# A hybrid encoder layer in split fp32 on one core: weight casts of the first pass placed behind the u of the block ahead, and three late row tiles normalised on GpSimd

## The chip, the core and the metric

The kernel runs on one core of a Trainium2 chip. The metric is the device time of one execution in microseconds (us). Three runs of the kernel before took 689.14, 689.45 and 689.67 us; their median is 689.45 us. A profile of one more execution was taken, and all rows below are from it.

## The reference

One layer with 1024 tokens of width 1024. `c` is a conditioning vector that gives a scale, a shift and a gate.

```python
mod = silu(c) @ w_ada + b_ada                       # shift, scale, gate: 1024 each
u = layer_norm(x) * (1 + scale) + shift             # [1024, 1024]
h = u @ w_in                                        # q, k, v, gate columns of two head groups
...
y = concat(fox(fq, fk, fv, ff) * silu(fg), stick_breaking(sq, sk, sv) * silu(sg)) @ w_out
out = layer_norm(2 ** 0.25 * x + gate * y) * ln_g + ln_b
```

## The kernel before, in words

All matrix products are done on TensorE (PE) with every fp32 operand split into two fp32r parts, a rounded one ("hi", names `uh`, `whi`, the first half of `hw`) and a remainder ("lo", names `ul`, `wlo`, the second half of `hw`); a product is hi·hi + hi·lo + lo·hi, so three matmuls. The order of PE and of the DMA queue on SP is the order of the code. ScalarE (ACT), VectorE (DVE) and GpSimd (POOL) get their order from a scheduler, which `with after(...)` (L83) can hold: an instruction in it is placed behind the ones named.

The width of 1024 is cut into 8 column blocks `kb`, the tokens into 8 row tiles `t` of 128. The rows of `x` are normalised per row tile; after that PE transposes 128x128 pieces so that a block of u lies with its width on the partitions.

**First pass** (L672 to L734, about 12 to 46 us of the span). It works on row tiles 0 to 3 (512 tokens) and goes through the blocks 0 to 7. Five sums grow side by side in PSUM, `st_q0`, `st_k0`, `st_g0`, `st_q1`, `st_k1` (`acc0`). For each block:

- `mod_terms(kb)` (L230): two DVE instructions per block, each the sum over one 128x1024 tile of `w_ada` columns times silu(c). They give `modc`, the scale and the shift of that block. The tiles `wss` are loaded by SP into three buffers.
- `u_turn` (L242): four transposes on PE into the PSUM tile `xT_early`.
- `u_round` (L248, L249): two ACT instructions. The first writes `uh` (rounded), the second puts the full u back into the PSUM tile.
- `u_rest` (L261): DVE writes `ul`, the full u less `uh`. After that `xT_early` is free for the next block's transposes. `in_turn` (L223) keeps the terms and the remainders on DVE in the order of the calls.
- `start_split` (L598, L599): the weights of the block, four pieces of 128 columns: ACT casts `raws` into the hi half of `hw`, POOL subtracts and writes the lo half.
- `start_steps` (L612, L615): PE. For blocks 2 to 6 the order is: eight matmuls that read `uh` (four with weight hi, four with weight lo), the four transposes of the next block, two more with `uh` for the fifth sum, and five with `ul`.

In the loop of block kb, the u of block kb+1 is held behind the ACT cast of the weights of block kb+1 (L685). The weights of block kb+2 are split in the loop of block kb (L706).

**Row tiles 4 to 7** are normalised near the end of the first pass: `norm_stats` (L193 to L211) has two BN_STATS and a BN_AGGR on DVE and two or three 128x1 instructions on POOL, `norm_x` (L214) is one 128x1024 instruction. By `NORM_ON` (L76) tiles 4 and 5 are normalised on ACT (L218), 6 and 7 on DVE (L217).

**Behind the first pass** PE makes the values of head pair 0 for row tiles 0, 1 and 2 (`v_first`, 24 matmuls of 128x256 each, L352 to L354), then the transposes of row tiles 4 to 7 for blocks 0 and 1 (`late_round`, L773), the values of row tile 3, and the **second pass**: the first three sums for tokens 512 to 1023, with u of block kb+2 made two blocks ahead. The values of row tile t are evicted in two halves (L360 on ACT, then L361 on DVE, then the same for the second half). Row tiles 0 and 2 share the PSUM tile `st_late`, so the matmuls of row tile 2 wait for the DVE eviction of row tile 0. The second pass's third sum `st_g0b` takes the PSUM buffer of `st_g0` and waits for its eviction (`evac_g`, L289 on ACT, L290 on DVE).

Then the attention runs with the remaining projections between its steps, and at the end the output projection with the last layer norm.

Of the kernel before, what the change touches and what calls it, by code (L numbers as in the profile page):

```python
# [16 lines left out]
NB = 8  # L17
# [10 lines left out]
def tile_hybrid_layer(  # L28
# [17 lines left out]
    nc = tc.nc  # L46
# [6 lines left out]
    def big(tag, bufs, name, dt=F32, shape=None):  # L53
        return sb.tile(shape or [P, 1024], dt, tag=tag, bufs=bufs, name=name)
# [4 lines left out]
    def pt_tile(name, dt=F32R, shape=None):  # L59
        return big("pt", 3, name, dt, shape or [P, 2, 1024])  # L60
# [12 lines left out]

    RING = 5
    WARM = (4, 1, 1, 0, 0)
    NORM_ON = {6: nc.vector, 7: nc.vector}  # L76
    FLOG = 4
    FROW = 8
    GATE = 10
# [3 lines left out]
    def after(*instructions):  # L83
        stack = ExitStack()
        for i in instructions:
            stack.enter_context(tc.issue_after(i.ins))
        return stack
# [29 lines left out]
    def ring_w(key):  # L117
        return [sb.tile([P, 528], F32R, tag=tag, bufs=RING, name=f"{tag}_{key}") for tag in ("whi", "wlo")]
# [33 lines left out]
    def load_ss(kb):  # L152
        t = sb.tile([P, 2, D], F32, tag="v", bufs=3, name=f"wss_{kb}")
        for a in ((0, 1), (1, 2)) if kb < 6 else ((0, 2),):
            nc.sync.dma_start(t[:, a[0]:a[1], :], w_ss[kb, :, a[0]:a[1], :])
        wss_sb.append(t)
# [38 lines left out]
    def ln_stats(src, name):  # L195
        st = sb.tile([P, 3, 6], F32, tag="st", bufs=3, name=f"st_{name}")[:, :2, :]
        nc.vector.bn_stats(st[:, 0, :], src[:, 0:512])
        nc.vector.bn_stats(st[:, 1, :], src[:, 512:1024])
        return ln_finish(st, name)
# [8 lines left out]
    def norm_stats(t):  # L208
        mv, rs = norm[t] = ln_stats(xt[t], f"a{t}")
        if t not in NORM_ON:  # L210
            nc.gpsimd.tensor_scalar(rs[:, 1:2], mv[:, 0:1], rs[:, 0:1], -1.0, op0=ALU.mult, op1=ALU.mult)  # L211

    def norm_x(t, a=0, b=D):
        mv, rs = norm[t]  # L214
        xs = xt[t][:, a:b]
        if t in NORM_ON:
            return NORM_ON[t].tensor_scalar(xs, xs, mv[:, 0:1], rs[:, 0:1], op0=ALU.subtract, op1=ALU.mult)  # L217
        return nc.scalar.activation(xs, xs, AF.Identity, scale=rs[:, 0:1], bias=rs[:, 1:2])  # L218
# [4 lines left out]
    def in_turn(make, *args):  # L223
        with after(*turn_of):
            turn_of[:] = [make(*args)]
        return turn_of[0]
# [6 lines left out]
    def mod_terms(kb, parts=(0, 1)):  # L233
        for i in parts:
            in_turn(mod_part, kb, i)
# [3 lines left out]
    def u_turn(kb, a=0, b=512, tp=None, tiles=None):  # L239
        tp = xT[kb, a] = tp or t_tile(f"xT_{kb}_{a}")  # L240
        for t in tiles or range(a // P, b // P):
            nc.tensor.transpose(tp[:, t * P - a:t * P - a + P], xt[t][:, kb * P:(kb + 1) * P], ident)  # L242
# [3 lines left out]
    def u_round(kb, a=0, b=512):  # L246
        full = xT[kb, a][:, :b - a]
        nc.scalar.activation(u_hi[kb][:, a:b], full, AF.Identity, scale=modc[:, kb, 0:1], bias=modc[:, kb, 1:2])  # L248
        return nc.scalar.activation(full, full, AF.Identity, scale=modc[:, kb, 0:1], bias=modc[:, kb, 1:2])  # L249

    def u_split(kb):
        full = raw_tile(f"u_full_{kb}")[:, :512]
        psum = xT.pop((kb, 0))[:, :512]
        s, b = (modc[:, kb, i:i + 1] for i in range(2))
        nc.scalar.activation(u_hi[kb][:, :512], psum, AF.Identity, scale=s, bias=b)
        last = nc.scalar.activation(full, psum, AF.Identity, scale=s, bias=b)
        nc.gpsimd.tensor_tensor(u_lo[kb][:, :512], full, u_hi[kb].bitcast(F32)[:, :512], op=ALU.subtract)
        return last
# [54 lines left out]
    def evac_m(p, m, ch, acc, heads=(0, 1)):  # L313
        if m == 0:
            evac_q(p, ch, acc, qst[p], heads)
        elif m == 1:
            return evac_k(p, ch, acc, kst[p], klo[p], heads)
        else:
            evac_g(p, ch, acc, sgt[p])
# [244 lines left out]
    raw_w, split, split_at, used, early_w = {}, {}, {}, [0], []  # L564
# [21 lines left out]
    def start_split(key):  # L586
        if key[0] == "h" or key[1] < 3:
            hi, lo = ring_w("st" + key[0] + str(key[1]))
        else:
            if key[1] == 3:  # L590
                early_w.append(pt_tile("hw_34"))
            elif key[1] == 5:
                early_w.append(pt_tile("hw_56"))
            home = (early_w[-1][:, (key[1] - 3) % 2, :] if key[1] < 7 else big("sg", 2, "hw_7", F32R))
            hi, lo = home[:, :512], home[:, 512:]
        split[key] = hi, lo
        h3, l3 = (t[:, :512].rearrange("p (m c) -> p m c", m=4) for t in (hi, lo))
        split_at[key] = (nc.scalar.copy(h3, raw_w[key]),  # L598
                         nc.gpsimd.tensor_tensor(l3, raw_w[key], h3.bitcast(F32), op=ALU.subtract))  # L599

    def start_steps(ns, accs, kb, a=0, b=512, parts=(0, 1), ends=None):
        first, last = ends or (kb == 0, kb == NB - 1)
        s = slice(a, b)
        w = {}
        for n in ns:
            hi, lo = split[("k", kb) if n < NW else ("h", kb // 4)]
            at = n if n < NW else kb % 4
            w[n] = hi[:, at * P:at * P + P], lo[:, at * P:at * P + P]
        if 0 in parts:
            for i in range(2):  # L610
                for n in ns:
                    nc.tensor.matmul(accs[n], w[n][i], u_hi[kb][:, s], start=(first and i == 0), stop=False)  # L612
        if 1 in parts:
            for n in ns:
                nc.tensor.matmul(accs[n], w[n][0], u_lo[kb][:, s], start=False, stop=last)  # L615
# [25 lines left out]
    rounded = u_split(0)  # L641
# [18 lines left out]
    def v0_load(n):  # L660
        if n == 0:
            home = sb.tile([P, 4, 512], F32R, tag="v", bufs=3, name="v0_home")
            v0_home.update({m: (home[:, 2 * m], home[:, 2 * m + 1]) for m in range(2)})
        v0_raw[n] = start_raw(1)
        nc.sync.dma_start(v0_raw[n], w_v[0, n])
# [6 lines left out]
    for kb in range(NB):  # L672
        last = kb == NB - 1
        if last:
            start_steps(ALL[:2], acc0, kb)
            for n in range(2):
                evac_m(*START[n], 0, acc0[n])
            start_steps(ALL[2:], acc0, kb)
            break
        start_steps(ALL[:4], acc0, kb, parts=(0,))  # L680
        if kb == 0:
            u_turn(2, tp=xt_early)
        elif kb > 1:
            u_turn(kb + 1, tp=xt_early)
        with after(split_at["k", kb + 1][0]):  # L685
            rounded = u_split(kb + 1) if kb == 0 else u_round(kb + 1)
        if kb == 0:
            with after(rounded):
                start_split(("h", 0))
            mod_terms(2)  # L690
        else:
            parts = range(2 if kb + 2 < NB else 0)
            mod_terms(kb + 2, parts[:1])
            rest = in_turn(u_rest, kb + 1)
            mod_terms(kb + 2, parts[1:])
        if kb == 0:
            start_steps(ALL[:4], acc0, kb, parts=(1,))
        elif kb == 1:
            start_steps(ALL[:4], acc0, kb, parts=(1,))
            for k in range(2):  # L700
                start_steps(ALL[4:], acc0, k)
        else:
            start_steps(ALL[4:], acc0, kb, parts=(0,))
            start_steps(ALL, acc0, kb, parts=(1,))
        if kb + 2 < NB:
            start_split(("k", kb + 2))  # L706
        if kb == 2:
            start_split(("h", 1))
        if kb + 5 < NB:
            load_ss(kb + 5)  # L710
            if kb == 0:
                load_w4(6, 2)
        if kb == 2:
            for n in range(2):
                v0_load(n)
            load_x(4)
            for n in range(2, 4):
                v0_load(n)
            for t in range(5, NB):
                load_x(t)  # L720
        if kb == 5:
            with after(*split_at["k", NB - 1]):
                for n in range(4):
                    v0_split(n)
            norm_stats(4)
            norm_stats(5)
            norm_x(4)
            norm_x(5)
        if kb == 6:
            with after(rest):  # L730
                for t in (6, 7):
                    norm_stats(t)
                    norm_x(t)
            make_v(0)  # L734
# [57 lines left out]
    rounded = late_round(1)  # L792
# [4 lines left out]
    for kb in range(NB):  # L797
        if kb + 2 < NB:
            rounded = late_round(kb + 2)
# [338 lines left out]
```

## Time and profile before

| what | value |
|---|---|
| median of three runs | 689.45 us |
| time of the profiled execution | 689.13 us |
| its span | 687.2 us |
| PE busy | 671.8 us (98%) |
| DVE busy | 488.3 us (71%) |
| ACT busy | 381.3 us (55%) |
| POOL busy | 403.2 us (59%) |
| first matmul of the values of row tile 0 | 46.31 us |
| first matmul of the sum `st_g0b` | 60.80 us |

The profiled execution lies 1.93 us above its span, and 0.32 us below the median. A row of the timeline has the start in us from the start of the span, the duration in us, the engine, the line, the operation, what is written from what is read, a count, and in brackets how long the engine had been idle and what released it. PEld is PE's weight load, SPq the issue of a DMA on SP.

### The profile page before, as it was taken

What the parts mean: (1) busy time and instruction counts of PE and PEld (TensorE: products, weight loads), DVE (VectorE), ACT (ScalarE), POOL (GpSimd) and SP (SyncE); (2) the same over time, 40 slices, a digit from 0 to 9 for tenths busy, and PEclk for the clock granted to TensorE, in tenths of its full rate; (3) what the DMA queues carried; (4) which work ended last, traced back from release to release, by engine and by line L of the source; (5) the groups of instructions that cost most, each with busy time, mean ns of one, the idle gap of its engine ahead of it and who ended that gap; (6) DMA issues with size and microseconds to landing.
All of it is one profiled execution on the core that took longest, in us unless ns stands there. A gap on an engine that the chain in (4) does not pass through costs nothing.

```text
span 687.2 us, 11196 instructions
## 1 busy us (share of the span) xinstructions
PE 671.8 (98%) x3709; PEld 571.2 (83%) x3709; DVE 488.3 (71%) x996; ACT 381.3 (55%) x857; POOL 403.2 (59%) x529
## 2 busy tenths in 40 slices
PE   8999999999999999999999999999999999999995
PEld 5788888788998888889988888889988878888885
DVE  6696769968668677777776675766676778785645
ACT  6566377756667666566665564655565666521000
POOL 5650179746447655556369878668785365655411
PEclk9999999999999999999999999999999999999998
DMA  9954422112102112112134455254352297143301
GB/s 335 409 221 170 152 74 76 40 26 55 40 9 70 40 54 55 40 50 58 36 104 128 161 162 166 80 176 146 116 163 72 60 353 300 59 174 106 118 31 61
DMA packets 45272, 81.54 MB, mean 119 GB/s; under 512 B 5216, under 2 KB 19360, under 8 KB 44960
## 3 DMA queue, kind: packets, MB, share of 16 engines
q1 hardware_dynamic: 43632, 76.54, 33.8%
q10 hardware_dynamic: 1584, 4.31, 1.9%
q8 instruction: 29, 0.48, 0.3%
q14 instruction: 27, 0.22, 0.1%
HBM read 60.34 MB, written 16.29 MB: 112 GB/s over the span
## 4 chain that ended last, share of the span: by engine, by line
PE 83%; DVE 6%; DMA 4%; ACT 3%; POOL 2%; issue 2%; DVEq 0%; POOLq 0%; ACTq 0%
PE m L296 9%; PE pv L526 9%; PE m L298 9%; PE m L297 9%; PE T L509 9%; PE S L458 4%; PE S L457 4%; PE o L901 4%; PE o L900 4%; PE o L899 4%; PE v L354 3%; PE v L352 3%; PE v L353 3%; DMA wss<-in_w_ss_dram 3%; PE st_late L612 1%
## 5 line engine op out<-in xcount | busy, mean ns | idle before, releaser
L296 PE MATMUL m<-uh,whi 128*128 128x512 f32 x304 | 125.0, 411 | 0.7 <-DVE kl L284 0.7
L512 DVE TENSOR_TENSOR pt<-T,pt 128x512 fp32r<-128x512 f32 (+2 forms) x192 | 103.1, 551 | 26.0 <-ACT pt L511 24.2
L298 PE MATMUL m<-uh,wlo 128*128 128x512 f32 x304 | 119.7, 394 | 0.0
L297 PE MATMUL m<-ul,whi 128*128 128x512 f32 x304 | 119.6, 394 | 0.0
L511 ACT CAST pt<-T 128x512 fp32r<-128x512 f32 (+2 forms) x192 | 88.6, 478 | 42.0 <-PE T L509 39.1
L492 POOL TENSOR_TENSOR be<-be,kp 128x127 f32<-128x127 f32 (+3 forms) x64 | 77.1, 1204 | 37.2 <-DVE kp L490 27.6
L486 DVE TENSOR_TENSOR_SCAN kp<-kp,floor 128x512 f32<-128x512 f32 (+2 forms) x64 | 65.1, 1018 | 27.6 <-ACT kp L479 25.4
L526 PE MATMUL pv<-pt,v 128*128 128x512 f32 x320 | 82.8, 388 | 0.3 <-DVE pt L512 0.3
L536 POOL TENSOR_TENSOR ty<-ty,sg 64x256 f32<-64x256 f32 x64 | 47.0, 734 | 42.6 <-DVE ty L535 18.3
L473 POOL TENSOR_SCALAR a<-a,l 128x1024 f32<-128x1024 f32 (+3 forms) x64 | 48.2, 752 | 39.7 <-DVE l L471 29.5
L298 PEld LDWEIGHTS m<-uh,wlo 128*128 128x128 f32 x304 | 57.1, 188 | 13.7
L457 PE MATMUL S<-k,q 128*128 128x512 f32 (+5 forms) x192 | 66.2, 346 | 0.2 <-DVE nm L465 0.2
L296 PEld LDWEIGHTS m<-uh,whi 128*128 128x128 f32 x304 | 57.2, 188 | 10.1 <-DVE kl L284 1.1
L458 PE MATMUL S<-kl,qz 128*128 128x512 f32 (+5 forms) x192 | 65.3, 341 | 0.0
L470 ACT ACTIVATE a<-a,nm 128x1024 f32<-128x1024 f32 (+3 forms) x64 | 49.8, 778 | 26.4 <-DVE nm L465 25.8
L297 PEld LDWEIGHTS m<-ul,whi 128*128 128x128 f32 x304 | 57.3, 189 | 7.9
L526 PEld LDWEIGHTS pv<-pt,v 128*128 128x128 f32 x320 | 55.4, 189 | 9.6 <-DVE pt L512 0.6
L479 ACT ACTIVATE kp<-S 128x128 f32<-128x128 f32 (+3 forms) x64 | 41.8, 652 | 33.7 <-PE S L458 31.3
L465 DVE CUSTOM_DVE_ANT_0 a<-S,fb 128x1024 f32<-128x1024 f32 (+3 forms) x64 | 48.2, 754 | 15.8 <-PE S L458 12.4
L431 ACT CAST qz<-q 64x128 fp32r<-64x128 f32 x128 | 37.3, 295 | 34.5 <-PE S L458 33.3
L352 PE MATMUL v<-whi_v,uh 128*128 128x256 f32 (+1 forms) x192 | 55.5, 289 | 0.0
L354 PE MATMUL v<-wlo_v,uh 128*128 128x256 f32 (+1 forms) x192 | 54.3, 283 | 0.3 <-POOL wlo_v L127 0.3
(290 smaller groups left out, 1625.0 us busy)
## 6 DMA issues: line engine op xcount, KB each, us to landing
raw<-in_w_qkg_dram SPq DMA_DIRECT2D x38, 256.0 KB, 2.6
wss<-in_w_ss_dram SPq DMA_DIRECT2D x12, 512.0 KB, 8.4
x<-in_x_dram SPq DMA_DIRECT2D x8, 512.0 KB, 6.8
k<-k SPq DMA_DIRECT2D x32, 128.0 KB, 2.3
wg<-in_w_gate_dram SPq DMA_DIRECT2D x8, 512.0 KB, 4.2
raw_o<-in_w_out_dram SPq DMA_DIRECT2D x16, 256.0 KB, 3.0
fb<-f_dr ACTq DMA_DIRECT2D x8, 512.0 KB, 4.2
wo_dr<-whi_o SPq DMA_DIRECT2D x16, 256.0 KB, 2.2
```

The source lines that it names most:

```text
L296: nc.tensor.matmul(acc, hi[:, c], u_hi[kt][:, s], start=(kt == 0), stop=False)
L297: nc.tensor.matmul(acc, hi[:, c], u_lo[kt][:, s], start=False, stop=False)
L298: nc.tensor.matmul(acc, lo[:, c], u_hi[kt][:, s], start=False, stop=(kt == NB - 1))
L352: nc.tensor.matmul(acc[:, :n], u_hi[kt][:, ts_], hi[:, s], start=(kt == 0), stop=False)
L354: nc.tensor.matmul(acc[:, :n], u_hi[kt][:, ts_], lo[:, s], start=False, stop=(kt == NB - 1))
L457: nc.tensor.matmul(S[:, s, :w], qst[p][h][:, qs], kst[p][h][:, ks], start=True, stop=False)
L458: nc.tensor.matmul(S[:, s, :w], z, klo[p][:, ks], start=False, stop=True)
L486: last_dve = nc.vector.tensor_tensor_scan(rv, rv, floor[:, :ke - lo], initial=0.0, op0=ALU.mult, op1=ALU.max)
L492: nc.gpsimd.tensor_tensor(be[:, :ke - 1], be[:, :ke - 1], kp[:, 1:ke], op=ALU.mult)
L511: nc.scalar.copy(hi[:, :n, qo:qo + P], t3)
L512: lows[:] = [nc.vector.tensor_tensor(lo[:, :n, qo:qo + P], t3, hi.bitcast(F32)[:, :n, qo:qo + P], op=ALU.subtract)]
L526: nc.tensor.matmul(acc2[:, :, q0:], vt[p][:, kb, h * P:(h + 1) * P], pt[:, :, q0:], start=(kb == 0), stop=(kb == last))
```

## The change

```diff
-    NORM_ON = {6: nc.vector, 7: nc.vector}
+    NORM_ON = {t: nc.gpsimd for t in (5, 6, 7)}
...
-        with after(split_at["k", kb + 1][0]):
+        with after(*split_at["k", kb + 1][:1] if kb < 2 else ()):
             rounded = u_split(kb + 1) if kb == 0 else u_round(kb + 1)
...
             parts = range(2 if kb + 2 < NB else 0)
-            mod_terms(kb + 2, parts[:1])
+            late = kb in (3, 4)
+            mod_terms(kb + 2, () if late else parts[:1])
             rest = in_turn(u_rest, kb + 1)
-            mod_terms(kb + 2, parts[1:])
+            mod_terms(kb + 2, parts if late else parts[1:])
...
-        if kb + 2 < NB:
-            start_split(("k", kb + 2))
         if kb == 2:
             start_split(("h", 1))
+        elif kb < 2:
+            start_split(("k", kb + 2))
+        elif kb + 2 < NB:
+            with after(rounded):
+                for k in ((4, 5) if kb == 3 else (kb + 2,)):
+                    start_split(("k", k))
```

Row tiles 5, 6 and 7 are normalised on POOL. From block 3 on, u no longer stands behind a weight cast; the weights of blocks 4 to 7 are split behind the u of the block ahead (4 and 5 behind the u of block 4, 6 behind that of 5, 7 behind that of 6). In the loops of blocks 3 and 4 the remainder (of blocks 4 and 5) stands ahead of both DVE sums of the next block (5 and 6). PE and SP keep their order; ACT, DVE and POOL have another one only between the u of block 4 and the eviction of `st_g0`, and from there on every engine has the same list as before.

Place 1 is ACT in the first pass, from the u of block 4 to that of block 6. The first number in a name is the block or pair (for `hw` the blocks whose weights it holds), the last only a tile's number; `raws_3` holds the weights of blocks 4 and 5, `raws_4` those of 6 and 7. Before:

```order
L598 CAST hw_34_321<-raws_3_248 128x512
L248 ACTIVATE uh_4_128<-xT_early_147,modc_140 128x512
L249 ACTIVATE xT_early_147<-xT_early_147,modc_140 128x512
L598 CAST hw_56_396<-raws_3_248 128x512
L598 CAST hw_56_396<-raws_4_296 128x512
L598 CAST hw_7_449<-raws_4_296 128x512
L248 ACTIVATE uh_5_129<-xT_early_147,modc_140 128x512
L249 ACTIVATE xT_early_147<-xT_early_147,modc_140 128x512
L248 ACTIVATE uh_6_130<-xT_early_147,modc_140 128x512
```

And now:

```order
L248 ACTIVATE uh_4_128<-xT_early_147,modc_140 128x512
L249 ACTIVATE xT_early_147<-xT_early_147,modc_140 128x512
L598 CAST hw_34_321<-raws_3_248 128x512
L598 CAST hw_56_396<-raws_3_248 128x512
L248 ACTIVATE uh_5_129<-xT_early_147,modc_140 128x512
L249 ACTIVATE xT_early_147<-xT_early_147,modc_140 128x512
L598 CAST hw_56_396<-raws_4_296 128x512
L248 ACTIVATE uh_6_130<-xT_early_147,modc_140 128x512
L249 ACTIVATE xT_early_147<-xT_early_147,modc_140 128x512
L598 CAST hw_7_449<-raws_4_296 128x512
```

The cast of block 4's weights moved from ahead of its u to behind it; the casts of blocks 6 and 7 moved from ahead of the u of block 5 to behind the u of blocks 5 and 6. POOL's four subtractions keep their order.

On DVE at the same place, the sums (L230, each with a row that reads its accumulator) and the remainders (L261). Before:

```order
L230 ISA wss_5_293,modc_140<-sc_all_111,wss_5_293,bss_sb_99 128x1024
L230 ISA modc_140 128x1
L261 TENSOR_TENSOR ul_4_136<-xT_early_147,uh_4_128 128x512
L230 ISA wss_5_293,modc_140<-sc_all_111,wss_5_293,bss_sb_99 128x1024
L230 ISA modc_140 128x1
L230 ISA wss_6_324,modc_140<-sc_all_111,wss_6_324,bss_sb_99 128x1024
L230 ISA modc_140 128x1
L261 TENSOR_TENSOR ul_5_137<-xT_early_147,uh_5_129 128x512
```

And now:

```order
L261 TENSOR_TENSOR ul_4_136<-xT_early_147,uh_4_128 128x512
L230 ISA wss_5_293,modc_140<-sc_all_111,wss_5_293,bss_sb_99 128x1024
L230 ISA modc_140 128x1
L230 ISA wss_5_293,modc_140<-sc_all_111,wss_5_293,bss_sb_99 128x1024
L230 ISA modc_140 128x1
L261 TENSOR_TENSOR ul_5_137<-xT_early_147,uh_5_129 128x512
L230 ISA wss_6_324,modc_140<-sc_all_111,wss_6_324,bss_sb_99 128x1024
L230 ISA modc_140 128x1
```

The remainders of blocks 4 and 5 went ahead of the first sum of blocks 5 and 6.

Place 2 is the eviction of the values of row tile 0 on DVE (`v_0` and `v_1` are the two halves, from `st_late`). Before:

```order
L189 BN_AGGR mv_a7_514<-st_a7_511 128x2
L217 TENSOR_SCALAR x_67_369<-x_67_369,mv_a6_505,rs_a6_507 128x1024
L361 TENSOR_TENSOR v_0_520<-st_late_548,v_0_520 128x128
L217 TENSOR_SCALAR x_67_369<-x_67_369,mv_a7_514,rs_a7_516 128x1024
L361 TENSOR_TENSOR v_1_521<-st_late_548,v_1_521 128x128
```

And now:

```order
L284 TENSOR_TENSOR kl_0_254<-st_k0_149,k_0_1_253 64x512
L189 BN_AGGR mv_a6_504<-st_a6_501 128x2
L361 TENSOR_TENSOR v_0_519<-st_late_547,v_0_519 128x128
L189 BN_AGGR mv_a7_513<-st_a7_510 128x2
L361 TENSOR_TENSOR v_1_520<-st_late_547,v_1_520 128x128
```

Both 128x1024 instructions are gone from between the evictions. On POOL they stand now behind the small instructions of row tiles 5 to 7 (`rs`), with nothing large of POOL behind them until the attention:

```order
L191 TENSOR_SCALAR rs_a5_474<-mv_a5_472 128x1
L192 TENSOR_TENSOR rs_a5_474<-rs_a5_474,mhalf_89 128x1
L217 TENSOR_SCALAR x_5_365<-x_5_365,mv_a5_472,rs_a5_474 128x1024
L191 TENSOR_SCALAR rs_a6_506<-mv_a6_504 128x1
L191 TENSOR_SCALAR rs_a7_515<-mv_a7_513 128x1
L192 TENSOR_TENSOR rs_a6_506<-rs_a6_506,mhalf_89 128x1
L192 TENSOR_TENSOR rs_a7_515<-rs_a7_515,mhalf_89 128x1
L217 TENSOR_SCALAR x_67_367<-x_67_367,mv_a6_504,rs_a6_506 128x1024
L217 TENSOR_SCALAR x_67_367<-x_67_367,mv_a7_513,rs_a7_515 128x1024
```

Three 128x1024 instructions came to POOL, and row tile 7 is the last of the three.

Place 3 is ACT behind the values of row tile 2, where the u of the second pass begins. Before:

```order
L360 CAST v_0_520<-st_late_548 128x2x64
L248 ACTIVATE uh_0_124<-xT_0_512_642,modc_140 128x512
L249 ACTIVATE xT_0_512_642<-xT_0_512_642,modc_140 128x512
L360 CAST v_1_521<-st_late_548 128x2x64
L248 ACTIVATE uh_1_125<-xT_1_512_652,modc_140 128x512
```

And now:

```order
L360 CAST v_0_519<-st_late_547 128x2x64
L360 CAST v_1_520<-st_late_547 128x2x64
L248 ACTIVATE uh_0_124<-xT_0_512_641,modc_140 128x512
L249 ACTIVATE xT_0_512_641<-xT_0_512_641,modc_140 128x512
L248 ACTIVATE uh_1_125<-xT_1_512_651,modc_140 128x512
```

The second half of the eviction of row tile 2 moved ahead of the first u of the second pass.

## The prediction

> **What bounds the kernel now.** I read the page first, then the chain of waits that ended last for 0 to 140 us, then the timelines of ACT, DVE, POOL and PE from 8 to 62 us, where the order of the built program changes.
>
> ```profile
> PE 671.8 (98%) x3709; PEld 571.2 (83%) x3709; DVE 488.3 (71%) x996; ACT 381.3 (55%) x857; POOL 403.2 (59%) x529
> PE 83%; DVE 6%; DMA 4%; ACT 3%; POOL 2%; issue 2%; DVEq 0%; POOLq 0%; ACTq 0%
> ```
>
> PE is busy for 98% of the span and holds 83% of the chain; what is not PE lies mostly in the first 60 us. There the chain shows (start, duration, what):
>
> ```profile
> 23.78 10.83 DMA wss<-in_w_ss_dram
> ...
> 51.83 0.81 DVE x L217
> 52.90 0.39 PE st_late L352
> ...
> 56.49 0.78 ACT uh L248
> ...
> 59.46 0.69 DVE ul L261
> ...
> 60.80 0.50 PE st_g0b L612
> ```
>
> First a load of scale and shift columns for blocks 6 and 7, then an inner wait behind DVE's normalisation of row tile 7, then the u of the second pass. From 60.80 us on the chain follows PE without a gap worth naming up to the attention (92 us). All engines have their old order from there, and each instruction waits for others of the same list, so I take what is gained at 60.80 as gained at the end: the sum has to be made for that one matmul.
>
> **Step 1, first pass, blocks 4 to 7.** ACT, DVE, PE and POOL before:
>
> ```profile
> 28.41 0.62 ACT L598 CAST hw<-raws 128x512 fp32r<-128x512 f32 x1 [3.08 <-DMA raws<-in_w_qkg_dram]
> 28.93 0.77 ACT L248 ACTIVATE uh<-xT_early,modc 128x512 fp32r<-128x512 f32 x1
> 29.61 0.74 ACT L249 ACTIVATE xT_early<-xT_early,modc 128x512 f32<-128x512 f32 x1
> ...
> 33.24 0.77 ACT L248 ACTIVATE uh<-xT_early,modc 128x512 fp32r<-128x512 f32 x1
> ...
> 37.94 0.78 ACT L248 ACTIVATE uh<-xT_early,modc 128x512 fp32r<-128x512 f32 x1 [3.28 <-DVE modc L230]
> ```
>
> ```profile
> 27.57 0.09 DVE L230 DVE_READ_ACCUMULATOR2_ANT modc<- 128x1 f32 x1
> 29.60 1.28 DVE L230 CUSTOM_DVE_ANT_0 wss<-sc_all,wss,bss_sb 128x1024 f32<-128x1024 f32 x1 [1.95 <-DMA wss<-in_w_ss_dram]
> ...
> 34.75 1.28 DVE L230 CUSTOM_DVE_ANT_0 wss<-sc_all,wss,bss_sb 128x1024 f32<-128x1024 f32 x1 [2.05 <-DMA wss<-in_w_ss_dram]
> ...
> 36.56 1.28 DVE L230 CUSTOM_DVE_ANT_0 wss<-sc_all,wss,bss_sb 128x1024 f32<-128x1024 f32 x1
> ```
>
> ```profile
> 27.19 0.60 PE L242 MATMUL xT_early<-ident,x 128*128 128x128 f32 x4
> 29.76 0.50 PE L612 MATMUL st_q<-uh,hw 128*128 128x512 f32 x1 [0.35 <-ACT uh L248]
> ...
> 31.73 0.60 PE L242 MATMUL xT_early<-ident,x 128*128 128x128 f32 x4
> ...
> 33.57 0.40 PE L615 MATMUL st_k<-ul,whi_sth 128*128 128x512 f32 x1
> ...
> 34.07 0.50 PE L612 MATMUL st_q<-uh,hw 128*128 128x512 f32 x1
> ...
> 38.83 0.44 PE L612 MATMUL st_q<-uh,hw 128*128 128x512 f32 x1
> ```
>
> ```profile
> 29.10 1.28 POOL L599 TENSOR_TENSOR hw<-raws,hw 128x512 fp32r<-128x512 f32 x1 [3.34 <-ACT hw L598]
> ```
>
> Block 4. Its terms are there at 27.66 and its transposes at 27.79, but ACT sits in the cast (28.41) until the weights land, and u starts at 28.93. Now u starts at 27.83 and ends at 29.25 (0.68 to the second instruction, which takes 0.74); the cast stands at 29.17 to 29.79 and POOL's half, 0.07 behind as before, at 29.86 to 31.14. So the weights are now last: PE starts the block at 29.85 instead of 29.76, and its four matmuls with weight lo, which would come at 30.89, wait until 31.19. With about 0.1 for the restart the transposes of block 5 come at 32.21 instead of 31.73. **PE loses 0.48 here.** From the transposes to the end of the block it takes 33.57 + 0.23 - 31.73 = 2.07, so block 5 starts at 34.28 instead of 34.07.
>
> Block 5. The remainder of block 4 now follows u at 29.28 and frees DVE for the first sum at 29.89; the load had landed by 29.60. A remainder, a sum and the start of the second sum take 36.56 - 34.75 = 1.81 in either order, and u follows the start of the second sum by 37.94 - 36.56 = 1.38: terms at 29.28 + 1.81 + 1.38 = 32.47. The transposes end at 32.81, so u of block 5 starts at 32.85 instead of 33.24, since two weight casts no longer stand ahead of it.
>
> Block 6. That u ends at 34.27, the remainder starts at 34.30, the first sum at 34.91 (its load landed by 34.75, so the remainder now fills a wait for that load), the second at 36.11, u at 37.49 to 37.51 instead of 37.94: **0.43 earlier**. PE would be done with block 5 at 34.28 + 1.86 + 2.07 = 38.21 and waits for that u in both kernels, so block 6 starts at 38.40 instead of 38.83. PE's loss in block 4 is thus swallowed by this wait. The subtractions for blocks 6 and 7 stand well ahead of their readers (36.1 and 40.8 against 39.3 and 42.9). Block 7 follows through the same chain of u, remainder, second sum and u, 0.43 earlier throughout.
>
> **Step 2, the wait inside the values.**
>
> ```profile
> 46.31 0.28 PE L352 MATMUL st_late<-v_home,uh 128*128 128x256 f32 x1
> ...
> 49.04 0.28 PE L354 MATMUL st_late<-v_w,uh 128*128 128x256 f32 x1
> ...
> 51.89 0.28 PE L354 MATMUL v<-v_w,uh 128*128 128x256 f32 x1
> ...
> 55.86 1.03 PE L242 MATMUL xT<-ident,x 128*128 128x128 f32 x8
> ...
> 59.93 0.71 PE L612 MATMUL st_late<-uh,whi_stk 128*128 128x512 f32 x2
> ```
>
> ```profile
> 50.44 0.27 ACT L360 CAST v<-st_late 128x128 fp32r<-128x128 f32 x1
> ...
> 56.06 0.27 ACT L360 CAST v<-st_late 128x128 fp32r<-128x128 f32 x1 [2.72 <-PE st_late L354]
> ...
> 57.83 0.27 ACT L360 CAST v<-st_late 128x128 fp32r<-128x128 f32 x1
> ```
>
> Row tile 0 is ready at 49.32, but ACT evicts it only at 50.44, behind the normalisation of row tile 5, and DVE's second half stands behind that of row tile 7 (51.83). PE has its next slot at 51.89 + 0.12 = 52.01 and starts at 52.90. In the new order ACT has one normalisation (row tile 4, ready with POOL, below) ahead, DVE none. ACT evicts at 48.93, DVE follows, and both halves are done by 50.9 even if DVE keeps its old pace; PE asks at 51.58. **The wait of 0.89 goes**, and 0.1 of restart with it: the transposes of row tiles 4 to 7 come at 55.86 - 0.43 - 0.99 = 54.44, 1.42 earlier.
>
> **Step 3, the three normalisations on POOL.** They are now late, if anything is.
>
> ```profile
> 39.97 2.55 POOL L670 TENSOR_TENSOR v_home<-raws,v_home 128x512 fp32r<-128x512 f32 x2 [4.53 <-ACT v_home L669]
> ...
> 45.97 0.26 POOL L211 TENSOR_SCALAR rs_a<-mv_a,rs_a 128x1 f32<-128x1 f32 x1
> ```
>
> ```profile
> 50.19 0.21 DVE L189 BATCH_NORM_AGGREGATE mv_a<-st_a 128x2 f32<-128x12 f32 x1
> ```
>
> ```profile
> L473 POOL TENSOR_SCALAR a<-a,l 128x1024 f32<-128x1024 f32 x8 | 9.0, 1126 | 8.6 <-DVE l L471 8.5
> L492 POOL TENSOR_TENSOR be<-be,kp 128x1023 f32<-128x1023 f32 x8 | 16.0, 1998 | 7.4 <-DVE kp L490 7.4
> L943 POOL TENSOR_TENSOR r<-r,lngb 128x320 f32<-128x320 f32 x1 | 0.9, 859 | 0.6 <-ACT r L942 0.6
> ```
>
> Block 7's weight half now ends on POOL at about 40.8, and the list from there to row tile 4's last small instruction takes 45.97 + 0.26 - 39.97 = 6.26 as before: 47.1. Row tile 5 follows until about 49.2. Row tile 7's statistics end on DVE no later than before (50.40); with four small instructions the last two normalisations begin by 51.9. Their duration is the unknown cost. The nearest row is L473: POOL, one tensor in place, a scalar from a column, 1.13 us. DVE's 0.81 (L217) is the bound below, POOL's two-tensor row with 2.00 the bound above. With 1.13 row tile 7 is ready at 54.1, and its transpose, the fourth, is due at about 54.7: **hidden, with some 0.6 us to spare**. A shorter one gains nothing; with 2.00 it is ready at 55.9.
>
> On this choice of engine the Trainium skill speaks against the change: "GPSIMD Engine Reference", section 4.1 Engine selection, wants elementwise work on VectorE, with GPSIMD about twice as slow for two inputs and roughly line-rate for one. Twice DVE's 0.81 would be an estimate of 1.62 by that page and would put row tile 7 at 55.1, so the sum would stay within 0.1 us; by its one-input clause it is the sum above.
>
> **Step 4, given back at the second pass.** From the transposes to the waiting matmul it was 60.80 - 55.86 = 4.94. Now the second half of row tile 2's eviction stands ahead of the first u. Row tile 2 ends at 54.60; ACT's first half follows at 54.64, DVE's at 54.93, ACT's second half at 55.25, u 0.16 later at 55.41. From there to the second remainder it was 59.46 - 56.49 = 2.97 with such a half in between (0.16), now 2.81: 58.22. The sum waited for follows 60.80 - 59.46 = 1.34 behind it: **59.56 instead of 60.80**. PE itself would be there at 59.0, so ACT and DVE bound this place.
>
> **The sum.** 0.43 + 0.99 - 0.18 = 1.24 us earlier at `st_g0b`. Against the profiled execution (span 687.2, 1.93 outside it) that is 687.89; that execution lay 0.32 below the median of the runs, so against the median it is 689.45 - 1.24 = 688.2, which I give. 0.2% of 689.45 is 1.38 us, about what a measurement of this kernel can tell from no change, so the forecast lies just inside.
>
> **The rivals.**
>
> *POOL's normalisation costs as much as its two-tensor row (2.00).* Row tile 7 is ready at 55.9, the first transposed block at 56.1, and u starts 0.7 later than in step 4: gain 0.5, 688.9. Against it: L473 is the same kind of instruction. Chance 0.10.
>
> *The first pass gains nothing*, because loads land later than in this execution (the chain has 10.83 us of that load) or weight lo comes late enough in block 4 to use up PE's slack of 0.2 behind block 5. Then step 1 is zero: gain 0.81, 688.6. Chance 0.12.
>
> *Step 4 gives nothing back and PE bounds.* Before, PE would have reached `st_g0b` at 59.93 + 0.47 = 60.40. If ACT and DVE keep up, all of 1.42 and this wait of 0.40 are gained: 1.82, 687.6. For it: both engines are idle in stretches here. Against: step 4's chain has no idle piece. Chance 0.15.
>
> *Slower: the normalisation of row tile 7 ends last.* If two column scalars and a subtraction run on POOL at the rate of L943 (859 ns for 320, so 2.75 for 1024), it is ready at 57.4, u starts at 57.6, 2.2 later than in step 4: 1.0 us slower, 690.4. It turns at a duration of 2.3, and is slower by 0.2% from about 2.95. Chance 0.08, of which 0.04 beyond 0.2%.
>
> That the change doesn't do what it says is excluded here by the order: the rows stand where the text puts them, and nothing else moved.
>
> **How the numbers follow.** The forecast has 0.55; its own range, with 0.3 for the spread of the runs and 0.3 for the latencies, is 687.6 to 688.8, and four tenths of it lie beyond 1.38. Faster: 0.22 + 0.15 = 0.37. Slower: 0.04, with 0.02 for what I don't see: 0.06. Same: 0.57. The range takes in the rivals on both sides but the slowest: 687.3 to 689.3.
>
> **What would show it.** Right: u of block 6 near 37.5; first matmul of the values near 45.9; no wait of PE for DVE between row tiles 1 and 2; L217 on POOL near 1.13 three times; `st_g0b` near 59.6, waiting for DVE. Wrong: PE's transposes at 54 us waiting for POOL; block 6 at 38.8; or the 1.2 us there at 60 us and not at the end.

## The result, and the profile after

Four runs of the changed kernel took 696.12 to 697.43 us with a median of 696.45; the kernel before, on the same chip, took 689.56 (689.14 to 689.92). The ratio is 1.0100 with an interval of 1.0085 to 1.0115: **slower by 1.0%, where 1.24 us faster was forecast**. The profiled execution took 697.43 with a span of 695.1.

The page's busy line of the changed kernel, and its shares of the chain:

```profile
PE 674.0 (97%) x3709; PEld 573.9 (83%) x3709; DVE 487.5 (70%) x994; ACT 380.6 (55%) x856; POOL 413.8 (60%) x531
PE 85%; POOL 4%; DVE 4%; ACT 3%; issue 2%; DMA 1%; SPq 0%; DVEq 0%; POOLq 0%; ACTq 0%
```

POOL has 10.6 us more than before, and twice its share of the chain. Three normalisations at the forecast 1.13 would be 3.4. The chain of waits that ended last shows where they stand:

```profile
50.12 2.44 POOL x L217
52.57 1.32 issue
53.89 0.40 POOL rs_a L191 x2
...
55.34 7.58 POOL x L217 x2
62.96 1.33 PE xT L242 x5
```

One is the 3.80 from 50.12, the other two fill 55.34 to 62.92 without a gap. PE's timeline shows who waited:

```profile
56.42 0.38 PE L242 MATMUL xT<-ident,x 128*128 128x128 f32 x2
59.18 0.33 PE L242 MATMUL xT<-ident,x 128*128 128x128 f32 x1 [2.38 <-POOL x L217]
62.96 1.33 PE L242 MATMUL xT<-ident,x 128*128 128x128 f32 x5 [3.45 <-POOL x L217]
63.94 0.56 PE L352 MATMUL v<-v_home,uh 128*128 128x256 f32 x1
64.30 0.41 PE L353 MATMUL v<-v_home,ul 128*128 128x256 f32 x1
...
66.38 0.28 PE L354 MATMUL v<-v_home,uh 128*128 128x256 f32 x1
66.49 0.28 PE L352 MATMUL v<-v_w,uh 128*128 128x256 f32 x1
...
68.82 0.46 PE L612 MATMUL st_g0b<-uh,whi_stk 128*128 128x512 f32 x1
```

The transposes of row tiles 6 and 7 each wait for POOL, 5.83 us in all: the prediction's sign of being wrong. Behind the second wait the values of row tile 3 begin with matmuls of 0.41 us where they take 0.28, up to 66.38. In the windows of PE (window, its length, busy time and count, granted clock, DMA share, GB/s) the clock falls there:

```profile
50.00:60.00 10.00, 7.13 (x59) 0.97 0.63 223
60.00:70.00 10.00, 7.04 (x40) 0.69 0.00 0
```

Before, both windows had 1.00. Four points in time, of the two profiles and of a second profile of the changed kernel (its repetition below):

| us from the start of the span | before | after | after, again |
|---|---|---|---|
| transposes of block 4 (`xT_early`) | 27.19 | 29.20 | 27.72 |
| first matmul of the values | 46.31 | 47.87 | 46.48 |
| transposes of row tiles 4 to 7 | 55.86 | 56.42 | 55.03 |
| first matmul of `st_g0b` | 60.80 | 68.82 | 67.44 |
| from there to the end of the span | 626.4 | 626.3 | 626.3 |

So the loss lies between the third and the fourth row: 12.4 us instead of 4.94. What is gained or lost at `st_g0b` is found at the end, as the prediction took it.

### The profile page after: what moved, and what is told of

Its sections match the earlier page's. It is cut to its first block, busy times and chain, and to the rows that moved or that the text cites. A ratio compares the mean times of both kernels' runs of the same rounds, so it can differ in the third digit from the quotient of the medians.

```text
span 695.1 us, 11197 instructions
## 1 busy us (share of the span) xinstructions
PE 674.0 (97%) x3709; PEld 573.9 (83%) x3709; DVE 487.5 (70%) x994; ACT 380.6 (55%) x856; POOL 413.8 (60%) x531
## 4 chain that ended last, share of the span: by engine, by line
PE 85%; POOL 4%; DVE 4%; ACT 3%; issue 2%; DMA 1%; SPq 0%; DVEq 0%; POOLq 0%; ACTq 0%
PE pv L526 9%; PE m L296 9%; PE m L298 9%; PE m L297 9%; PE T L509 8%; PE S L457 4%; PE S L458 4%; PE o L906 4%; PE o L905 4%; PE o L904 4%; PE v L354 4%; PE v L352 4%; PE v L353 3%; POOL x L217 1%; PE st_q L612 1%
## 5 line engine op out<-in xcount | busy, mean ns | idle before, releaser
L473 POOL TENSOR_SCALAR a<-a,l 128x1024 f32<-128x1024 f32 (+3 forms) x64 | 48.2, 754 | 38.3 <-DVE l L471 30.2
```

## The experiments

**Which form of the normalisation is dear on POOL?** Two kernels append single TENSOR_SCALAR instructions behind POOL's last one in the kernel before, on a tile that nobody else uses (an addition of work; the outputs are as before).

```diff
+    ts(scr, scr, two, one, op0=ALU.subtract, op1=ALU.mult)
+    ts(scr[:, :512], scr[:, :512], two, one, op0=ALU.subtract, op1=ALU.mult)
...
+    ts(scr, scr, two, one, op0=ALU.mult, op1=ALU.mult)
+    ts(scr, scr, two, one, op0=ALU.mult, op1=ALU.add)
+    ts(scr, scr, two, 1.0, op0=ALU.subtract, op1=ALU.mult)
...
+    ts(scr, scr, two, None, op0=ALU.mult)
```

> The kernel before, with twelve POOL instructions on a scratch tile added behind its last one (they lengthen the run and change no output). All are TENSOR_SCALAR in place on 128x1024 fp32 but two narrower ones. Theory A, the subtraction is what costs: every row with subtract near 3.8 us (as the three normalisations of the changed kernel, 3.78 to 3.80), every row with mult and add near 1.13, whatever the number of column scalars. Theory B, the second column scalar costs: the three kinds with two columns (subtract and mult, mult and mult, mult and add) near 3.8, all others near 1.13. Theory C, it is neither but the neighbours (DVE at work on the same memory, or the tile): all rows near 1.13 here, since DVE is idle then. Width: if it is a cost per element, 512 takes near 1.95 and 256 near 1.05.

POOL's timeline in the first of them:

```profile
684.10 3.81 POOL L1083 TENSOR_SCALAR scr<-scr,mhalf,ones 128x1024 f32<-128x1024 f32 x1
688.01 2.08 POOL L1084 TENSOR_SCALAR scr<-scr,mhalf,ones 128x512 f32<-128x512 f32 x1
...
691.51 1.20 POOL L1086 TENSOR_SCALAR scr<-scr,mhalf,ones 128x1024 f32<-128x1024 f32 x1
692.81 1.20 POOL L1087 TENSOR_SCALAR scr<-scr,mhalf,ones 128x1024 f32<-128x1024 f32 x1
694.10 3.70 POOL L1088 TENSOR_SCALAR scr<-scr,mhalf 128x1024 f32<-128x1024 f32 x1
...
706.98 2.85 POOL L1093 TENSOR_SCALAR scr<-scr,mhalf 128x1024 f32<-128x1024 f32 x1
```

Subtract and multiply takes 3.81 with two columns (L1083) and 3.70 with one (L1088); multiply·multiply and multiply·add with two columns take 1.20 (L1086, L1087). So it is the pair of operations, not the number of columns, and not a neighbour, since DVE was idle here (its last row ends at 684.01). A multiply with no second operation takes 2.85 (L1093), more than with one, which no theory had.

> The kernel before, with eleven POOL instructions on a scratch tile behind its last one (they lengthen the run and change no output), all in place, 128x1024 but two of 512. From the first such run: subtract 3.63 to 3.81 with a second operation, 2.85 alone; mult with mult or add 1.11 to 1.20; mult alone 2.85. Theory S, pairs made of mult and add are quick and whatever else is slow: add and mult, mult and mult, add and add near 1.2; mult and subtract, max and min near 3.7; one operation alone near 2.85 whichever it is. Rival F, only mult in first place is quick: add and mult, add and add near 3.7, and mult and subtract near 1.2. The row at 512 for mult and add near 0.7, for mult alone near 1.6 if the cost goes with the elements.

The second kernel asked for the rule behind it. Its first three rows are add·multiply, multiply·subtract and add·add:

```profile
683.73 1.19 POOL L1083 TENSOR_SCALAR scr<-scr,mhalf,ones 128x1024 f32<-128x1024 f32 x1
685.03 3.80 POOL L1084 TENSOR_SCALAR scr<-scr,mhalf,ones 128x1024 f32<-128x1024 f32 x1
688.93 3.82 POOL L1085 TENSOR_SCALAR scr<-scr,mhalf,ones 128x1024 f32<-128x1024 f32 x1
```

Add·add, at 3.82, was expected quick by the theory that blames the subtraction, so that theory is too narrow; max·min took 3.78. Quick were multiply·multiply, multiply·add and add·multiply. That these run a path of their own is a reading of the list; why they do stays open.

**Which part of the change costs?** The first pass alone (normalisations on the engines of before) and the normalisations alone (first pass of before):

```diff
-    NORM_ON = {t: nc.gpsimd for t in (5, 6, 7)}
+    NORM_ON = {6: nc.vector, 7: nc.vector}
```

> The changed kernel with the normalisations back where they were (5 on ACT, 6 and 7 on DVE), so the new order of casts and remainders alone. Theory 1, the whole loss is the three normalisations on POOL and the first pass gains what was forecast: 0.43 us below the kernel before, the values of row tile 0 at 45.9 instead of 46.31. Rival, the new order is itself part of the loss (PE waits for the weights of block 4 and does not get it back): 0.2 to 1.5 us above the kernel before, values later than 46.5.

688.08 us (687.55 to 689.63) against 689.47: ratio 0.9982, interval 0.9973 to 0.9991. **Faster by 1.4 us with no normalisation on POOL**, where 0.43 was expected. DVE's timeline says why the wait of 0.89 went here too:

```profile
50.68 0.29 DVE L361 TENSOR_TENSOR v<-st_late,v 128x128 fp32r<-128x128 f32 x1
51.30 0.29 DVE L361 TENSOR_TENSOR v<-st_late,v 128x128 fp32r<-128x128 f32 x1 [0.33 <-ACT v L360]
51.61 1.70 DVE L217 TENSOR_SCALAR x<-x,mv_a,rs_a 128x1024 f32<-128x1024 f32 x2
```

With the new first pass the scheduler itself puts the eviction of row tile 0 (L361) ahead of both normalisations (L217).

> The kernel before with row tiles 5, 6 and 7 normalised on POOL and nothing else changed. Theory 1: all of the loss is here, 6.9 us and the 0.4 that the order gained, so 7.0 to 7.5 above the kernel before; POOL's three rows at 3.8 each, PE's transposes waiting for the third. Rival, the order is part of the loss: 5.5 to 6.7 above.

696.25 us (695.81 to 696.68), ratio 1.0094, interval 1.0079 to 1.0110. That is 6.78 above the kernel before, between the two expectations and close to the changed kernel's 6.89: the loss is here. POOL's L217 has three rows of 3.8, and PE waits for two of them:

```profile
56.99 0.33 PE L242 MATMUL xT<-ident,x 128*128 128x128 f32 x1 [1.76 <-POOL x L217]
60.77 1.33 PE L242 MATMUL xT<-ident,x 128*128 128x128 f32 x5 [3.45 <-POOL x L217]
```

**Only the form exchanged.** POOL computes x·r + (-mean·r) with multiply and add, from the second column that ACT's form uses already (L211, one small instruction more for each row tile):

```diff
-        if t not in NORM_ON:
+        if NORM_ON.get(t) is not nc.vector:
             nc.gpsimd.tensor_scalar(rs[:, 1:2], mv[:, 0:1], rs[:, 0:1], -1.0, op0=ALU.mult, op1=ALU.mult)
...
-            return NORM_ON[t].tensor_scalar(xs, xs, mv[:, 0:1], rs[:, 0:1], op0=ALU.subtract, op1=ALU.mult)
+            return NORM_ON[t].tensor_scalar(xs, xs, rs[:, 0:1], rs[:, 1:2], op0=ALU.mult, op1=ALU.add)
```

> The changed kernel, with POOL computing x times rs plus (-mean times rs), so mult and add with two columns of one tile in place of subtract and mult with columns of two tiles; three 128x1 rows on POOL come with it (0.27 each). Theory A (the subtraction costs): rows near 1.13 to 1.2, the time 1.0 to 1.3 below the kernel before, as forecast at first. Theory B (the second column costs): rows near 3.8, time as the changed kernel, 6.9 to 7.5 above the kernel before.

688.20 us (687.90 to 688.67), ratio 0.9981, interval 0.9973 to 0.9990, 1.27 below before. POOL:

```profile
48.71 1.19 POOL L217 TENSOR_SCALAR x<-x,rs_a 128x1024 f32<-128x1024 f32 x1
...
52.34 1.19 POOL L217 TENSOR_SCALAR x<-x,rs_a 128x1024 f32<-128x1024 f32 x1
...
53.87 1.20 POOL L217 TENSOR_SCALAR x<-x,rs_a 128x1024 f32<-128x1024 f32 x1
```

Row tile 7 is ready at 55.07. PE's eight transposes from 54.64 take 1.25 where they took 1.03 before, so about 0.2 of waiting is left. It costs nothing here, since ACT is busy with row tile 2's eviction and not free for u until 55.62:

```profile
54.84 0.27 ACT L360 CAST v<-st_late 128x128 fp32r<-128x128 f32 x1 [1.96 <-PE st_late L354]
55.46 0.27 ACT L360 CAST v<-st_late 128x128 fp32r<-128x128 f32 x1 [0.36 <-DVE v L361]
55.62 0.79 ACT L248 ACTIVATE uh<-xT,modc 128x512 fp32r<-128x512 f32 x1
```

With the operation near the price that I had given it (1.19 for 1.13), the total of the sum comes out; its parts are taken up below.

**Was the late start of the first profile the change's doing?** The changed kernel once more, nothing edited:

> The changed kernel once more, beside the next two on the same chip. By the sum over its own rows (block 4 to the second pass) it should be 6.0 above the kernel before, and 6.9 was measured; the profiled execution had lost 1.6 to 2.0 ahead of block 4, where nothing was changed. Theory 1: the start varies from run to run, so 695.3 to 696.6. Rival: the start is later in this kernel in every run, so 696.3 or more and a profile with block 4's transposes again later than 28.5.

696.45 us (695.90 to 696.78), ratio 1.0101, interval 1.0086 to 1.0116; block 4's transposes start at 27.72 (table above). Both expectations allow the time; the start decides for the first. The 29.20 belongs to that one execution, the slowest of the eight, and is no part of the loss that all of them show.

**One slow normalisation instead of three**, for row tile 5; 6 and 7 on DVE:

```diff
+    NORM_ON = {5: nc.gpsimd, 6: nc.vector, 7: nc.vector}
```

> The changed kernel with row tile 5 alone on POOL, in the slow form (3.8), and 6 and 7 on DVE. POOL is free of it at about 51.9, its small instructions for 6 and 7 end at about 53.6, DVE normalises 6 at 53.7 and 7 behind an eviction of row tile 2 at about 55.2 to 55.9, and the fourth transpose comes near 56.0 instead of 54.7. Theory 1 (only what lies on the path to that transpose counts): 1.0 to 1.3 of the gain of 1.3 is lost, so 0.4 below to 0.2 above the kernel before. Rival (the slow instruction also holds up DVE or ACT beside it): DVE's rows between 48 and 52 us get longer, and the time is 0.5 or more above.

689.26 us (688.74 to 691.12), ratio 1.0001, interval 0.9992 to 1.0010. That is the first expectation. PE waits 1.07, for row tile 7:

```profile
53.29 0.81 DVE L217 TENSOR_SCALAR x<-x,mv_a,rs_a 128x1024 f32<-128x1024 f32 x1
55.31 0.29 DVE L361 TENSOR_TENSOR v<-st_late,v 128x128 fp32r<-128x128 f32 x1 [1.21 <-ACT v L360]
55.52 0.80 DVE L217 TENSOR_SCALAR x<-x,mv_a,rs_a 128x1024 f32<-128x1024 f32 x1
56.38 0.76 PE L242 MATMUL xT<-ident,x 128*128 128x128 f32 x5 [1.07 <-DVE x L217]
```

POOL's 3.80 for row tile 5 (48.56 to 52.36) holds up the small instructions of row tiles 6 and 7 until 54.14, and DVE normalises row tile 7 only behind an eviction of row tile 2 (L361). DVE's rows beside POOL's slow one take what they take in the first pass alone (L198 0.68 and 0.67, L284 0.69 in both, L361 0.29 in both), so the slow form does not slow the neighbour; it costs by its place in the queue.

**What does the clock add?** Filler matmuls (their sum is thrown away) keep PE at work while it waits for POOL:

```diff
     v_first(2, late_acc[:, 1, :])
+    busy(26, late_acc[:, 1, :])
```

> The changed kernel with 26 matmuls of 128x512 on PE between the values of row tile 2 and the transposes that wait for POOL; they write a PSUM tile already evicted and change no output. They fill some 6 us of the wait. Theory: after the wait PE runs at a lower granted clock for a few us (0.69 between 60 and 70 us), which costs 1.3 to 1.7 on top of the wait; with PE kept at work the clock stays near 1.0 and the time is 0.8 to 1.6 below the changed kernel. Rival: the clock there comes from something else, so the time is the same or up to 0.5 longer, since the last fillers may overrun the wait.

711.84 us (710.54 to 712.55), ratio 1.0318, outside both expectations: my mistake of size. A filler takes 0.87 us, not 0.23, and 26 of them (22.6 us) overran the wait. Six fit:

> The changed kernel with six filler matmuls behind the values of row tile 2, at 0.87 us each (as measured with 26 of them) 5.2 us, which fit into the wait for GpSimd. Theory (the wait itself also costs clock: TensorE's granted clock falls behind an idle stretch of some 6 us): the granted clock between 50 and 70 us is near 1.0, from the last transposes of the late row tiles to the second pass's first matmul of st_late it takes 4.1 us instead of 5.5, and the time is about 1.0 to 1.5 us below the changed kernel's 696.45, so 695.0 to 695.5. Rival (the longer way there is the chain of ACT and DVE, not the clock): no shorter than in the changed kernel, 696.5; if the fillers delay the transposes, 697.

694.89 us (694.69 to 695.60), 5.58 above the kernel before on the same chip, where the repetition lay 6.94 above: 1.36 less. PE:

```profile
56.02 5.42 PE L176 MATMUL st_late<-ident 128*128 128x512 f32 x12 [1.30 <-DVE v L361]
61.28 1.04 PE L242 MATMUL xT<-ident,x 128*128 128x128 f32 x8
...
66.05 0.50 PE L612 MATMUL st_g0b<-uh,whi_stk 128*128 128x512 f32 x1
```

Counted from block 4's transposes, these come no earlier than in the repetition (33.95 here, 33.86 there for the one that ends the wait), but from there to `st_g0b` it takes 4.77 instead of 5.86, at a granted clock of 1.00 from 50 to 70 us, where the repetition had 0.90 and 0.76. So some 1.1 of the loss at this place is clock, not waiting.

**A price in between.** The quick form's kernel with each POOL normalisation in halves, one subtract·multiply (2.08), one multiply·add (0.77): 2.85 for a row tile, near the 2.75 of my slower rival.

```diff
...
+                ha, hb = xt[t][:, a:(a + b) // 2], xt[t][:, (a + b) // 2:b]
+                nc.gpsimd.tensor_scalar(ha, ha, mv[:, 0:1], rs[:, 0:1], op0=ALU.subtract, op1=ALU.mult)
+                return nc.gpsimd.tensor_scalar(hb, hb, rs[:, 0:1], rs[:, 1:2], op0=ALU.mult, op1=ALU.add)
...
```

> The kernel of e4 with each GpSimd normalisation in two halves of 512 columns: the first as subtract and mult (2.08 by e1), the second as mult and add (0.77 by e5), so 2.85 for each row tile, between the quick form (1.20) and the slow one (3.80). It tries the price that the prediction gave its slower rival, 2.75, which it put at 690.4. Theory 1 (all three durations add up, since row tile 5's also holds up the small instructions of row tile 6, which stand behind it on GpSimd): row tile 5 from 48.7 to 51.6, row tile 6 from about 53.0 to 55.8, row tile 7 to 58.7; st_g0b at 63.9 to 64.6, some 3 to 3.6 us later than before: 692.5 to 693.1. Theory 2 (as the prediction's slower rival: only the last of the durations counts beyond its turning point of 2.3): 690.4 to 690.8.

691.39 us (690.69 to 694.19) against 689.31, ratio 1.0038, interval 1.0025 to 1.0051: between both theories. POOL's order (of the profile taken again, below) shows what both had missed:

```profile
53.20 2.09 POOL L219 TENSOR_SCALAR x<-x,mv_a,rs_a 128x512 f32<-128x512 f32 x1
55.28 0.26 POOL L211 TENSOR_SCALAR rs_a<-mv_a,rs_a 128x1 f32<-128x1 f32 x1
55.51 2.08 POOL L219 TENSOR_SCALAR x<-x,mv_a,rs_a 128x512 f32<-128x512 f32 x1
57.58 1.52 POOL L220 TENSOR_SCALAR x<-x,rs_a 128x512 f32<-128x512 f32 x2
```

The transposes of blocks 0 and 1 read only the first 256 columns, so each waits for the first half alone, and the second halves of row tiles 6 and 7 come last, where PE waits for neither. So what lay on the path was 2.85 for row tile 5 and 2.08 for each of the others. The profiled execution was the slowest of the six, and I took another:

> The kernel of e10 once more, for another profiled execution: that of e10 lay 2.8 above the median of its runs, with the transposes of block 4 at 29.43 and a granted clock of 0.83 between 60 and 70 us. Theory 1 (the late start is one execution's, as in the changed kernel's first profile, and the rest is as profiled): the transposes of block 4 at 27.1 to 27.7, from them to st_g0b 36.3 as before, the time 692.2 to 692.6. Theory 2 (whether the clock falls behind a wait of some 2 us also differs between executions): a granted clock near 1.0 between 55 and 70 us, from the transposes of block 4 to st_g0b about 35, and the time near 691.

690.65 us; block 4's transposes at 27.32, `st_g0b` at 62.14, the granted clock 1.00. In the first of the two, with waits of the same length (0.43 and 1.97), it had been 0.83 from 60 to 70 us. So the late start was one execution's, as theory 1 has it, and theory 2 holds as well: behind waits of this length the clock falls in some executions only.

**And the kernel before, for its start:**

> The kernel before once more, for another profile. Theory 1 (when the first pass's block 4 starts differs between executions of one kernel, by what the loads ahead of it take): its transposes at 27.0 to 27.7, as in the five profiled kernels with the usual start, and from them to st_g0b 33.6. Rival (the change delays the start by some 0.3): at 27.0 to 27.2, below all of the changed kernels.

689.54 us, but block 4's transposes at 29.39: neither expectation. The late start thus comes in both kernels. PE's timeline shows a wait of 1.06 for row tile 2 at 12.27 (none in the first profile), and behind it transposes of 1.05 instead of 0.60:

```profile
12.27 0.33 PE L242 MATMUL xT_early<-ident,x 128*128 128x128 f32 x1 [1.06 <-ACT x L218]
...
17.34 1.05 PE L242 MATMUL xT_early<-ident,x 128*128 128x128 f32 x4
...
29.39 0.60 PE L242 MATMUL xT_early<-ident,x 128*128 128x128 f32 x4
...
46.73 0.28 PE L352 MATMUL st_late<-v_home,uh 128*128 128x256 f32 x1
```

The granted clock from 15 to 20 us is 0.66 here, in the first profile after and in the first of the halves, and 1.00 in the other eleven profiles. In these three the wait for row tile 2 is 0.82 to 1.06, in the eleven 0.69 at most, so the late start goes with a long wait; that the wait brings the low clock was not tried. What matters more: the kernel before loses only 0.42 of those 2.2 us by the values (46.73 against 46.31).

## Why the prediction was wrong

**Step 3 failed, and alone set the sign.** It put POOL's normalisation at "1.13", after L473, with DVE's 0.81 below and "2.00 the bound above". It takes 3.80, 3.4 times the value and outside the bounds. "L473 is the same kind of instruction" was the error: L473 multiplies twice, L217 subtracts and multiplies, and the name TENSOR_SCALAR in the profile does not tell the two apart; the code does. The two forms by themselves (3.81, 1.20) and in place (3.80, 1.19 with nothing else exchanged) settle it. The rows of before had no subtracting TENSOR_SCALAR on POOL, so the upper end should have stayed open, and not stood at another operation's price. By the rows here the quick pairs take 1.3 to 1.5 times DVE's 0.81 (itself a subtract·multiply), a single operation 3.4 to 3.5 times, and the slow pairs 4.5 to 4.7 times. The Trainium skill's "GPSIMD Engine Reference", section 4.1 Engine selection, which I had quoted against the change, prefers VectorE and calls GPSIMD "roughly line-rate" for one input. Its direction is right; its size fits the quick pairs at best.

**The slower rival had the right mechanism, but not all of it**, and its price and its chance (0.08) were wrong. I had given it 2.75 from a two-tensor row, and no such likeness gives the measured number. By its own sum, which counts the last two normalisations from 51.9, a price of 3.80 would cost 3.05 us. The repetition has 6.11 (39.72 from block 4's transposes to `st_g0b`, against 33.61 before). What it left out first is row tile 5: the small instructions of row tiles 6 and 7 stand on POOL behind its 3.80, so the last two normalisations begin 26.23 behind block 4's transposes and not 24.71, 1.5 later. The other 1.6 lie between the end of row tile 7's normalisation and `st_g0b`, 5.92 where the sum has 4.35, and some 1.1 of them are clock.

The halves at 2.85 gave 2.08 more than before, at 3.80 it is 6.9. From the halves' second profile to the repetition, both from block 4's transposes on, row tile 7's first half or whole is ready 3.5 later (30.27 and 33.80) and `st_g0b` comes 4.9 later (34.82 and 39.72): nearly one for one, and the half clock on top, some 1.1 by the fillers.

I had no term for the clock. On it the Trainium skill's "TensorE: Matmul & The Clock Gate", section What's actually happening, says half rate after at least one idle window of some 3.4 us, and full rate again after at least one busy window of that length. The traces agree on the second: the slow matmuls last 3.42 us in the changed kernel (62.96 to 66.38), 3.41 in its repetition, 3.58 in the first profile of the halves and 6.01 with the normalisations alone. On the first, two waits of 2.40 in all were enough in one execution of the halves and not in another.

**Step 2 was right in size**: from the first matmul of the values to the transposes 8.55 in the changed kernel, 9.55 before, so 1.00 against 0.99. "In the new order ... DVE none" is true of this kernel but names more than was needed: the first pass alone, with DVE's normalisations kept, has 8.55 as well, and so have the normalisations alone (54.85 - 46.30). With either half of the change the eviction comes in time. So nothing had to move to POOL for it.

**Step 1 was right for a start like the quoted one, and not beyond.** From the transposes of block 4 to the values it takes 18.67 in the changed kernel, against 19.12: 0.45 for a forecast of 0.43. But the new order keeps 18.66 to 18.76 for every start, since there PE itself loses its time in block 4 (waits of 0.42 for ACT's cast and 0.16 for POOL's half; from its transposes to those of block 5 it takes 5.03 instead of 4.54, 0.49 more where 0.48 was forecast) and the chain of u, remainder and sums follows PE. The old order is bound by the load for block 6 (DVE waits 2.05 for it with the usual start, 1.69 with the late one) and swallows a late start: 17.34 from 29.39. So with a late start the new first pass loses (47.87 against 46.73). My rival that the first pass gains nothing thought of late loads; it is late matmuls that undo it. In the seven usual starts profiled with the new order the values begin at 45.99 to 46.48, in the four with the old at 46.21 to 46.53: a gain of 0.1 on the means. The few runs of the first pass alone that lie 1.5 above the others (689.56 and 689.63 among 688.0) fit a late start by their granted clock, 0.995 as in the late profile of before and 0.997 to 0.998 in the others, but weren't profiled.

**Step 4 was right**, in size and cause: 5.12 from the transposes to `st_g0b` with the quick form (54.64 to 59.76), 4.94 before, so 0.18 given back; and both halves of row tile 2's eviction stand ahead of u, as forecast, each row 0.2 later than forecast by the start (27.41 for 27.19). With the first pass alone the second half comes behind u and nothing is given back (54.91 to 59.85).

**The spare of 0.6 in step 3 was not there** even at 1.19: row tile 7 was ready 27.66 behind block 4's transposes, not 26.91, since POOL had to wait for DVE's statistics and for the small instructions of both row tiles. Two of these (L211, 0.27 and 0.26) come with the quick form alone.

**The sum** was 1.24; with the quick form the time is 1.27 lower. That is closer than the parts deserve: step 1 gives 0.1 on the means, and in the profiles `st_g0b` comes only 1.04 earlier (59.76 against 60.80). Part of the agreement is luck.

## What to carry to other kernels

A duration taken from another row holds only for the same operations, not for the same opcode: look up both ALU operations of the row in the code, and where no row has that pair, leave the upper bound open and make the slow case a rival with weight. On POOL, write a normalisation as x·r + b and not as (x - m)·r; here that alone turned 1.0% slower into 0.2% faster, though the first pass alone, with no work moved, gave the same. A gain ahead of a wait that swallows delays (here the load for block 6) should be tried with a later start too before it is counted.

## What the runs showed of the hardware

- POOL's TENSOR_SCALAR on 128x1024 fp32 in place: multiply·multiply, multiply·add, add·multiply 1.05 to 1.20 us; one operation alone (multiply, add, subtract) 2.77 to 2.85; pairs with subtract in either place, add·add, max·min 3.63 to 3.82. At 512 columns 0.77 (multiply·add), 1.57 (multiply alone), 2.08 (subtract·multiply).
- PE's granted clock fell to 0.50 behind 5.2 to 5.8 us of waiting in all three profiles that had it (0.66 to 0.76 on the mean of 60 to 70 us), and behind 2.4 in one of two. The slow matmuls behind the wait lasted 3.4 to 6.0 us.
- Near 15 us of the span it fell in three of the fourteen profiles, of either kernel and of the halves, each with a wait of 0.82 or more ahead. The first profile after and its repetition both begin block 0's matmuls at 14.28; with the slow stretch block 4's transposes come at 29.20, without it at 27.72.
